# First stage of a two-layer trunk: the modulation of the first layer loaded into the region of v, part of it multiplied on ScalarE and summed in fp32 on TensorE

## The chip, the core and the metric

The kernel runs on one core of one Trainium2 chip. The metric is device time in microseconds (us) of one execution. The kernel before has three runs. The profile shown is of one further execution.

## What is computed

The reference runs two layers, each a token mixer followed by a dense MLP, on x of 1024 tokens by 1024 features in fp32. Ahead of every one of the four sub-layers the input is modulated by a vector c (1024 values) that is the same for all tokens:

```python
def ada_mod(c, w, b):
    m = jax.nn.silu(c) @ w + b                    # w: 1024 x 3072
    shift, scale, gate = jnp.split(m, 3, axis=-1)
    return shift[:, None, :], scale[:, None, :], 1.0 + gate[:, None, :]

h = x * (1.0 + scale) + shift
y = mixer_a(h, ...)        # first layer: uv = gelu(h @ w_in + b_in); u, v = split(uv); ...
x = layer_norm(ALPHA * x + gate * y, ln_g, ln_b)
```

Only the very beginning matters here: `silu(c) @ w` for shift and scale of the first sub-layer, `h`, and the first half of the columns of v = gelu(h @ w_in + b_in).

## The kernel before

**Numbers.** Nearly all matrix products run in the type fp32r. An fp32 operand is split into a high part (a rounded copy) and a low part (the difference), and a product is three matmuls (high times high, high times low, low times high). `split` (L105 to L108) makes the two parts: the copy on ScalarE (A), the difference on VectorE (V).

**The first stage** is the block with `ada0` in `mixer_a` (L495 to L575). It does four things.

1. *The modulation*, `mods(h)` (L502): for each half h of the columns (512 of shift and 512 of scale at once), eight row blocks of 128 rows of `ada_w`, each 512 KB, are loaded into tiles `adaw` with six buffers. VectorE multiplies block k by column k of silu(c) and adds it to the accumulator `adaacc` (L509 for the first block, L511 for the others). The accumulator is then split into `adahi` and `adalo`, and `mod_cols` (L115) sums it over its 128 partitions on TensorE: 16 matmuls against two columns of ones (L119, L120) into a PSUM bank `psa`, once for scale and once for shift. VectorE adds the bias (L124); the result, a few columns, scales and shifts h.
2. *h transposed*, `build_hT` (L221): for a feature block k and up to four row tiles of x, TensorE transposes the tiles into a PSUM bank `pst` (L227), ScalarE applies the modulation (L232) and the result is split into high and low part `hT`.
3. *The weights*, `v_unit` (L466): 512 KB of `a_w_in` are loaded and split into `winv_hi` and `winv_lo`.
4. *The product*, `v_sum(c, i, k)` (L469): three matmuls of 128 x 512 for row tile i and feature block k into the PSUM bank `psv` of that tile. Six banks exist (`mm`); two more (`tr`) serve the transposes and `psa`.

Row tiles are taken in three groups: tiles 0 to 3, tiles 4 and 5, tiles 6 and 7. The feature blocks 0 to 3 need half h=0 of the modulation, the blocks 4 to 7 need half h=1. So the order on TensorE is: group 0-3 with blocks 0 to 3 (48 matmuls), group 4-5 with blocks 0 to 3 (24), then the same two groups with blocks 4 to 7 (48 and 24), then group 6-7 with all eight blocks (48). Each of these sums ends in `v_end` (L478): bias on VectorE, gelu on ScalarE, statistics on VectorE, written into `vz`, the region that holds v for all eight row tiles (8 x 1024 fp32 values per partition).

TensorE has nothing to multiply until the first modulation is there. A burst of 26 matmuls without use (`warm`, L513 to L516) runs from the arrival of block 4 of the first half.

**What sets the order.** A scheduler orders the instructions of each engine ahead of the run: program order is their priority, and an instruction that is marked with `keep_in_program_order` isn't moved against it. In the first stage before, the burst and the transpose of `rows` (L548) are marked; the transposes of x, the low parts and the accumulation on VectorE are not. All loads of the stage are issued by SyncE (SP). A buffer of a pool (or of a tag in it) is taken again when its last reader is done: `adaacc_0`, `adaacc_1` and the x tile 7 share one buffer (tag `gate`).

The rows of ln_g, ln_b, the biases (`rows`, L541 to L544) are loaded between the first x tiles and the second half's blocks, and transposed once (`row_cols`, L546). The bias of the modulation, `ada_b`, is loaded at the start beside c (L74), and both are transposed together (L79).

## Time and profile before

| | us |
|---|---|
| runs | 2681.38, 2685.55, 2686.34 (median 2685.55) |
| the profiled execution | 2684.56 |
| its span in the trace | 2682.9 |

The span runs from the first to the last instruction that the profile shows; 1.66 us of the profiled execution lie outside it. Its mean granted TensorE clock is 0.997 of full speed.

In the answers of the trace, PE is the matmul part of TensorE and PEld its weight loads, which overlap; DVE is VectorE, ACT is ScalarE, SPq the queue of SyncE. A row of the timeline has the start, the duration of the merged run of instructions, engine, line, operation, output <- input, count, and in brackets the idle time before it with what ended that. A row of the windows has the stretch, its length, the busy time of each engine with its count of instructions, the granted clock of TensorE, the share of the DMA engines that was busy, and GB/s.

### The profile page before, as it was taken

To read this page: it belongs to the slowest core of one execution; us is meant where nothing else is said; L and a number is where in the kernel's file an instruction comes from. 1 tells how busy PE (TensorE), PEld (TensorE's weight loads), DVE (VectorE), ACT (ScalarE), POOL (GpSimd) and SP (SyncE) were. 2 spreads that over 40 slices of the span, in tenths; PEclk is the share of its full clock that TensorE was granted. 3 is DMA by queue.
4 is the path that set the end of the run, shared out by engine and by line. 5 is a ranking of instruction groups with operands and counts; after the bars stand their busy time and mean duration, and the time that the engine had idled before them with its cause. 6 is when DMAs were issued, how large, how long until landed. Compare 5 with 4: busy or idle time off the path is not lost.

```text
span 2682.9 us, 36963 instructions
## 1 busy us (share of the span) xinstructions
PE 2646.9 (99%) x13204; PEld 2188.1 (82%) x13204; DVE 1981.9 (74%) x3582; ACT 1382.0 (52%) x2626; POOL 104.4 (4%) x189
## 2 busy tenths in 40 slices
PE   7999999999999999999999999999999999999998
PEld 6888878878888888888888888888877788888887
DVE  5896798787888888555557777776658966677877
ACT  3364475555444564433436666666656655553432
POOL 0000000000000001111110000000010000000000
PEclk9999999999999999999999999999999999999999
DMA  7643347677967645655565554555783654485562
GB/s 276 187 144 102 118 151 242 212 231 263 352 208 257 214 162 196 212 195 179 183 207 157 157 135 131 136 145 140 237 213 113 204 199 157 145 316 190 181 207 83
DMA packets 335069, 505.29 MB, mean 188 GB/s; under 512 B 51692, under 2 KB 168852, under 8 KB 334884
## 3 DMA queue, kind: packets, MB, share of 16 engines
q1 hardware_dynamic: 318500, 444.20, 52.0%
q0 software_dynamic: 16384, 58.73, 6.1%
q8 instruction: 103, 1.69, 0.3%
q14 instruction: 82, 0.67, 0.1%
HBM read 365.92 MB, written 136.92 MB: 187 GB/s over the span
## 4 chain that ended last, share of the span: by engine, by line
PE 69%; issue 17%; DVE 6%; DMA 4%; ACT 2%; POOL 2%; SPq 0%; POOLq 0%; DVEq 0%; ACTq 0%
PE psd L1015 19%; PE psua L853 9%; PE psk L1445 7%; PE psq L1445 6%; PE psuc L853 4%; PE psd_wout L391 3%; PE pv L1614 3%; PE psu L640 3%; PE sc L1534 3%; PE psv L475 3%; DMA adaw<-in_ada_w_dram 3%; PE psub L853 2%; PE pT L1587 1%; POOL v L1321 1%; PE psoa L1818 1%
## 5 line engine op out<-in xcount | busy, mean ns | idle before, releaser
L853 PE MATMUL psua<-right,left 128*128 128x512 f32 x1536 | 365.1, 391 | 1.6 <-ACT part L858 1.2
L1015 PE MATMUL psd<-rhi,lhi 128*128 128x512 f32 x896 | 349.7, 390 | 0.0
L1015 PE MATMUL psd<-rlo,lhi 128*128 128x512 f32 x896 | 348.8, 389 | 0.0
L1015 PE MATMUL psd<-rhi,llo 128*128 128x512 f32 x896 | 348.6, 389 | 0.0
L853 PEld LDWEIGHTS psua<-right,left 128*128 128x128 f32 x1536 | 286.3, 188 | 65.6 <-ACT part L858 3.6
L1556 ACT ACTIVATE p<-p,stat 128x128 f32<-128x128 f32 (+1 forms) x384 | 168.7, 441 | 97.1 <-DVE stat L1554 97.1
L1015 PEld LDWEIGHTS psd<-rhi,lhi 128*128 128x128 f32 x896 | 168.2, 188 | 35.8 <-ACT part L884 0.9
L1015 PEld LDWEIGHTS psd<-rhi,llo 128*128 128x128 f32 x896 | 168.2, 188 | 35.0
L1015 PEld LDWEIGHTS psd<-rlo,lhi 128*128 128x128 f32 x896 | 168.2, 188 | 34.6
L853 PE MATMUL psuc<-right,left 128*128 128x512 f32 x768 | 188.7, 392 | 1.1 <-ACT part L858 1.1
L853 PEld LDWEIGHTS psuc<-right,left 128*128 128x128 f32 x768 | 142.9, 188 | 33.4 <-ACT part L858 2.6
L108 DVE TENSOR_TENSOR pTlo<-pT,pThi 128x512 fp32r<-128x512 f32 (+1 forms) x160 | 99.2, 620 | 76.0 <-ACT pThi L107 75.0
L107 ACT CAST left<-ws 128x512 fp32r<-128x512 f32 x128 | 79.3, 621 | 143.4 <-DVE ws L777 104.6
L108 DVE TENSOR_TENSOR llo<-lraw,lhi 128x1024 fp32r<-128x1024 f32 x112 | 136.1, 1217 | 2.3 <-ACT lhi L107 2.3
L108 DVE TENSOR_TENSOR left<-ws,left 128x512 fp32r<-128x512 f32 x128 | 87.9, 688 | 66.1 <-ACT left L107 63.8
L144 DVE SCALAR_TENSOR_TENSOR adaacc<-adaw,silu_c,adaacc 128x512 f32<-128x512 f32 x140 | 104.4, 746 | 39.4 <-DMA adaw<-in_ada_w_dram 38.7
L1445 PE MATMUL psk<-form_L,wqk_hi 128*128 128x512 f32 x384 | 127.1, 412 | 0.5 <-DVE qlo L108 0.5
L1445 PE MATMUL psq<-form_L,wqk_hi 128*128 128x512 f32 x384 | 126.4, 410 | 0.0
L107 ACT CAST lhi<-lraw 128x1024 fp32r<-128x1024 f32 x112 | 117.1, 1047 | 7.1 <-PE psd L1015 3.3
L1344 PE MATMUL psv<-vrhi,form_S 128*128 128x512 f32 x384 | 119.9, 390 | 0.8 <-ACT vrhi L107 0.5
L1554 DVE CUSTOM_DVE_ANT_0 p<-sc,bias 128x128 f32<-128x128 f32 (+1 forms) x384 | 113.5, 345 | 6.6 <-PE sc L1534 6.2
L107 ACT CAST pThi<-pT 128x512 fp32r<-128x512 f32 (+1 forms) x160 | 84.7, 530 | 61.5 <-PE pT L1587 44.5
(333 smaller groups left out, 6072.6 us busy)
## 6 DMA issues: line engine op xcount, KB each, us to landing
lraw<-forms SPq DMA_DIRECT2D x112, 512.0 KB
adaw<-in_ada_w_dram SPq DMA_DIRECT2D x160, 256.0 KB
up<-in_mlp_w_up_dram SPq DMA_DIRECT2D x64, 512.0 KB
forms<-s SPq DMA_DIRECT2D x128, 256.0 KB
rraw<-in_mlp_w_down_dram SPq DMA_DIRECT2D x64, 512.0 KB
forms<-part SPq DMA_DIRECT2D x96, 256.0 KB
v<-vs POOLq DMA_DIRECT2D x48, 512.0 KB, 3.6
vraw<-in_b_w_qkv_dram SPq DMA_DIRECT2D x42, 512.0 KB
```

The costliest lines, as they stand in the source:

```text
L107: first = A.copy(hi, src) if hi_engine is A else hi_engine.tensor_copy(hi, src)
L108: return first, lo_engine.tensor_tensor(lo, src, hi, op=ALU.subtract)
L144: ins = V.scalar_tensor_tensor(acc[:], raw[:], silu_c[:, k : k + 1], acc[:], ALU.mult, ALU.add)
L391: T.matmul(p[:], stat[a][:, k, o : o + P], u[b][:, w], start=n == 0, stop=n == count - 1)
L475: T.matmul(sums[i][:], hT[half][a_][:, k, o : o + P], units[c, k // 2][b_][:, n : n + HALF], start=k + a_ + b_ == 0, stop=k == KD - 1 and ...
L640: T.matmul(p[:], wu[a_][:, k * P : (k + 1) * P], hT[half][b_][:, k, :], start=k + a_ + b_ == 0, stop=k == KD - 1 and a_ == 1)
L853: T.matmul(acc, w[:, a, k, :], right[p][:, b, k, :], start=p in (1, 2, 5) and k + a + b == 0, stop=k == 3 and a == 1, skip_group_check=True)
L1015: ins = T.matmul(sums[kind, m][:], l[a][:, k, m * P : (m + 1) * P], r[b][:, k, :], start=p in (1, 5, 2, 3) and kp + k + a + b == 0, stop=k ...
L1344: T.matmul(acc, rows[:, m * P : (m + 1) * P], cols_, start=p in (1, 2, 5) and kp + k + a + b == 0, stop=kp == 1 and k == 1 and a == 1, ski ...
L1445: T.matmul(p[:], wu[a][:, k * P : (k + 1) * P], h_op(k, half, b), start=k + c_ == 0, stop=k == KD - 1 and c_ == 2)
L1554: V.tensor_tensor_reduce(out=pr, in0=banks[e][:, sl], in1=st["bias"][:, width - w :], scale=-0.125, scalar=3e38, op0=ALU.add, op1=ALU.min, ...
L1556: A.activation(pr, pr, AF.Exp, bias=nm, scale=-1.0, accum_out=l)
```

## The change

- In the first half, all eight blocks of `ada_w` are loaded into `vz[:, k]`, which is free at that time, so no load waits for a buffer. In the second half the blocks 0 to 5 go to the `adaw` buffers and 6 and 7 to `vz[:, 0]` and `vz[:, 1]`. The weights `winv` 2 and 3 are loaded into `vz[:, 2]` and `vz[:, 3]`.
- In the first half, blocks 6 and 7 are multiplied by their column of silu(c) on ScalarE, in place, and go to TensorE as they are. Blocks 0 to 5 stay on VectorE. The second half stays on VectorE with all eight blocks.
- `total` sums over the partitions in fp32: 8 matmuls of a 128 x 128 block against one column of ones, for each of block 6, block 7 and the accumulator in the first half (24 in all), and for the accumulator in the second half (8). The split of the accumulator (four instructions for each half) and the 16 matmuls of `mod_cols` for each half are gone. `mod_cols` is still used by later stages.
- The burst has 18 matmuls in place of 26 and starts with block 0 in place of block 4.
- `ada_b` is loaded behind the eight blocks and transposed by itself between the sums; the loads of `rows` and their transpose move to the end of the stage.
- The transposes of x, the low parts of h, and VectorE's accumulation of the second half are kept in program order. `in_turn` puts the transposes of a feature block two steps ahead of its matmuls, and the groups 0-3 and 4-5 follow each other in one sequence. The second half's loads of x tiles 0 to 3 come ahead of `winv` 2 and 3.

```diff
-    cols_c = cst.tile([P, KD + 64], F32, name="cols_c")
-    cols_b = cols_c[:, KD : KD + 64]
+    cols_c = cst.tile([P, KD], F32, name="cols_c")
+    cols_b = cst.tile([P, 64], F32, name="cols_b")
+    one = cst.tile([P, 1], F32, name="one")
...
-        nc.sync.dma_start(rows_c[KD : KD + 64, :], ada_b.rearrange("i s (q p) -> (i s) q p", p=P)[:, 0 : 2 * KD, :])
...
-            split(hi, lo, h[:], hi_engine=hi_engines[k % 2])
+            ins = split(hi, lo, h[:], hi_engine=hi_engines[k % 2])
+            if pin_lo:
+                tc.keep_in_program_order(ins[1])
...
+            def in_turn(*runs):
+                todo = [(i0, n, k) for i0, n, ks in runs for k in ks]
+                gens = {(i0, n): rows_of(i0, n)(ks) for i0, n, ks in runs}
+                def rows(m):
+                    if m < len(todo):
+                        next(gens[todo[m][:2]])
+                rows(0)
+                rows(1)
+                yield
+                for m, (i0, n, k) in enumerate(todo):
+                    for i in range(i0, i0 + n):
+                        v_sum(0, i, k)
+                    yield
+                    rows(m + 2)
...
                 def mods(h, between=()):
+                    p = bank("tr", f"psa_{h}")
+                    def total(t, first, last):
+                        for part in range(2):
+                            for k in range(4):
+                                at = 8 * part + 2 * k
+                                T.matmul(p[:, at : at + 1], t[:, part, k * P : (k + 1) * P], one[:],
+                                         start=first and part + k == 0, stop=last and part + k == 4, skip_group_check=True)
                     for k in range(KD):
-                        raw = ada0.tile([P, 2, HALF], F32, name=f"adaw_0_{h}_{k}", tag="adaw", bufs=6)
+                        if h and k < 6:
+                            raw = ada0.tile([P, 2, HALF], F32, name=f"adaw_0_{h}_{k}", tag="adaw", bufs=6)[:]
+                        else:
+                            raw = vz[:, k - 6 * h, :].rearrange("p (t n) -> p t n", t=2)
...
+                        if h == 0 and k > 5:
+                            A.activation(raw, raw, AF.Copy, scale=silu_c[:, k : k + 1])
+                            total(raw, k == 6, False)
...
-                        if h == 0 and k == 4:
-                            A.copy(warm, raw[:, 0, :])
-                            for _ in range(26):
+                        elif k == 0:
+                            tc.keep_in_program_order(A.copy(warm, raw[:, 0, :]))
+                            for _ in range(18):
...
-                    hi, lo = (ada0.tile([P, 2, HALF], F32R, name=f"ada{m}_{h}", tag="adaw", bufs=6) for m in ("hi", "lo"))
+                    if h == 0:
+                        nc.sync.dma_start(rows_b[0:64, :], ada_b.rearrange("i s (q p) -> (i s) q p", p=P)[:, 0 : 2 * KD, :])
+                        pt = bank("tr", "rows_bt")
+                        tc.keep_in_program_order(T.transpose(pt[:, 0:P], rows_b[:], ident[:]))
+                        tc.keep_in_program_order(V.tensor_copy(cols_b[:], pt[:, 0:64]))
+                    total(acc[:], h == 1, True)
...
                 mods(0)
                 x_cols(0, range(4))
+                turns = in_turn((0, 4, first_ks), (4, 2, first_ks))
                 for kp in range(2):
+                    next(turns)
                     v_unit(0, kp)
...
+                then = {n: [lambda: next(turns)] for n in (1, 3, 5, 6, 7)}
                 mods(1, then)
-                x_cols(1, range(6))
+                x_cols(1, range(4))
+                for kp in (2, 3):
+                    v_unit(0, kp, vz[:, kp, :])
+                run(turns)
+                x_cols(1, (4, 5))
                 nc.sync.dma_start(vbias[:], a_b_in[0, D : 2 * D].partition_broadcast(P))
+                row_loads()
+                run(in_turn((0, 4, last_ks), (4, 2, last_ks)))
+                row_cols()
```

More of the change, by code (lines that the diff above doesn't have):

```diff
@@ L219, in in_pair, with build_hT @@
         return lambda k: tuple(t[:, k, :] for t in pair)
-    def build_hT(j, half, tiles, place, ks=range(KD), pinned=False, hi_engines=(A, V), name=None):
+    def build_hT(j, half, tiles, place, ks=range(KD), pinned=False, hi_engines=(A, V), name=None, pin_lo=False):
         name, n_cols = name or f"{j}_{half}", len(tiles) * P
@@ L569, in mixer_a @@
             later(ada_steps(0, GATE, 4) + ada_steps(1, MODS + GATE, 4))
-            gen = rows_of(6, 2)(range(KD))
-            for k in range(KD):
-                advance(gen, k, (6, 7))
-                tick()
+            for n, _ in enumerate(in_turn((6, 2, range(KD)))):
+                if n:
+                    tick()
             for i in (6, 7):
```

63 lines of the change are left out of this document (27 added, 36 removed).

## The prediction

> **What bounds the kernel now.** I read the page first, then the stage by windows, then the three engines' timelines in the first 50 us, then the clock.
>
> ```profile
> span 2682.9 us, 36963 instructions
> ...
> PE 2646.9 (99%) x13204; PEld 2188.1 (82%) x13204; DVE 1981.9 (74%) x3582; ACT 1382.0 (52%) x2626; POOL 104.4 (4%) x189
> ```
>
> TensorE is busy in all but 36 us (2682.9 - 2646.9). A microsecond that the start gives back is kept only if TensorE is packed behind it, so I cut the start into stages:
>
> ```profile
> 8.00:14.00 6.00, 1.14 (x3) 0.95 (x4) 5.51 (x5) 0.62 (x1) 0.00 (x0) 1.00 1.04 380
> 14.00:20.00 6.00, 6.00 (x20) 4.72 (x19) 4.63 (x5) 1.15 (x3) 0.00 (x0) 1.00 1.05 406
> 20.00:26.30 6.30, 5.92 (x40) 5.17 (x38) 3.12 (x6) 4.55 (x6) 0.00 (x0) 0.87 0.95 299
> 26.30:45.90 19.60, 19.02 (x82) 14.92 (x81) 15.21 (x18) 8.05 (x16) 0.00 (x0) 0.95 0.90 336
> 45.90:52.60 6.70, 6.15 (x34) 5.18 (x33) 2.07 (x6) 3.06 (x6) 0.00 (x0) 0.70 0.52 168
> 52.60:72.30 19.70, 19.18 (x82) 15.27 (x81) 9.62 (x17) 9.33 (x18) 0.00 (x0) 0.93 0.60 184
> 72.30:74.50 2.20, 1.08 (x7) 0.56 (x5) 1.91 (x4) 1.92 (x5) 0.00 (x0) 1.00 0.00 0
> ...
> 97.20:212.00 114.80, 114.80 (x535) 95.78 (x534) 101.37 (x172) 52.11 (x77) 0.00 (x0) 1.00 0.55 168
> ```
>
> The 115 us behind the stage are full, so what the stage gains or loses should reach the end one for one. The stage itself has a **front** (to 26.3, the first useful matmul), a first block of 72 matmuls (to 45.9), a **gap** of 6.7 us in which TensorE only sums and transposes, a second block of 72 (to 72.3), and a short gap of 2.2. Until 20 us the DMA engines are full (1.04 and 1.05). What ends the front shows on DVE, ACT and PE:
>
> ```profile
> 9.65 5.26 DVE L511 SCALAR_TENSOR_TENSOR adaacc<-adaw,silu_c,adaacc 128x1024 f32<-128x1024 f32 x4 [0.16 <-DMA adaw<-in_ada_w_dram]
> 15.56 2.60 DVE L511 SCALAR_TENSOR_TENSOR adaacc<-adaw,silu_c,adaacc 128x1024 f32<-128x1024 f32 x2 [0.65 <-DMA adaw<-in_ada_w_dram]
> 18.85 1.29 DVE L108 TENSOR_TENSOR adalo<-adaacc,adahi 128x512 fp32r<-128x512 f32 x2 [0.69 <-ACT adahi L107]
> ```
>
> ```profile
> 12.19 0.62 ACT L513 CAST hT<-adaw 128x512 fp32r<-128x512 f32 x1 [5.64 <-DMA adaw<-in_ada_w_dram]
> 18.20 1.14 ACT L107 CAST adahi<-adaacc 128x512 fp32r<-128x512 f32 x2 [5.39 <-DVE adaacc L511]
> 19.99 1.05 ACT L107 CAST winv_hi<-winv_raw 128x1024 fp32r<-128x1024 f32 x1 [0.66 <-DMA winv_raw<-in_a_w_in_dram]
> ```
>
> ```profile
> 12.86 8.57 PE L516 MATMUL warm<-hT,ones_r 128*128 128x512 f32 x26 [6.83 <-ACT hT L513]
> ...
> 22.75 0.25 PE L119 MATMUL psa<-ones_r,adahi 128*128 128x2 f32 x1
> 22.86 0.25 PE L120 MATMUL psa<-ones_r,adalo 128*128 128x2 f32 x1
> 22.97 0.66 PE L227 MATMUL pst<-ident,x 128*128 128x128 f32 x4
> 23.80 0.66 PE L227 MATMUL pst<-ident,x 128*128 128x128 f32 x4 [0.17 <-DVE ada L124]
> 24.67 1.97 PE L227 MATMUL pst<-ident,x 128*128 128x128 f32 x8 [0.22 <-ACT h L232]
> 26.29 0.78 PE L475 MATMUL psv<-winv_hi,hT 128*128 128x512 f32 x1
> ```
>
> The chain: the last modulation block (its DVE step starts at 15.56 + 1.30 = 16.86, so it has landed by then), the split on ACT and DVE (to 20.1), the sums `psa`, held back by the burst, which ends at 21.4, and 3.2 us from the end of `psa` (22.86 + 0.25 = 23.1) to the first `psv` at 26.29.
>
> **The change, part by part.**
>
> *Loads at once.* Sizes:
>
> ```profile
> adaw<-in_ada_w_dram SPq DMA_DIRECT2D x16, 512.0 KB
> x<-in_x_dram SPq DMA_DIRECT2D x16, 256.0 KB
> ```
>
> The DMA engines are full already, so loading at once moves no more bytes per microsecond; it takes one x load of 256 KB from ahead of blocks 6 and 7. At 0.38 to 0.41 MB per us that is 0.67 us: block 6 lands at 14.9, block 7 at 16.2. `winv` comes at 20.0 as before, having the same bytes ahead of it. `ada_b`, now behind the eight blocks, should land with block 7, ahead of its use.
>
> *Two blocks on ScalarE.* ACT needs about 1.05 for 128x1024 (the `winv_hi` row): block 6 done at 15.95, block 7 at 17.25. DVE, at 1.30 a block, would have ended block 7 at 17.5, so this alone gives some 0.2. It adds 16 matmuls.
>
> *The sum in fp32.* No row shows an fp32 matmul that isn't a transpose. The nearest rows are `psa`: 22.75 to 22.86, 0.11 us from one to the next at full clock. Below, I bound an fp32 one by the same 0.11; above, by the four products of two two-part operands, 0.44, and by twice that at half clock, 0.88. I take **0.18**, under the 0.22 of two loads, near the low row since only one column is streamed.
>
> [...]
>
> *The burst.* 18 matmuls from block 0, which lands four blocks of some 1.35 ahead of block 4 (12.19, the ACT row): near 7. The 26 took 8.57, so 18 take 6 to 7 and end near 14. The sums no longer wait for it, but TensorE then idles. The granted clock:
>
> ```profile
> 21.00:24.60 3.60, 3.29 (x26) 2.72 (x25) 2.23 (x4) 1.85 (x4) 0.00 (x0) 1.00 0.97 297
> 24.60:28.00 3.40, 3.33 (x12) 3.04 (x13) 2.23 (x4) 3.10 (x7) 0.00 (x0) 0.51 0.88 275
> ...
> 45.00:48.50 3.50, 3.02 (x20) 2.40 (x18) 2.09 (x5) 1.14 (x2) 0.00 (x0) 1.00 0.00 1
> 48.50:52.00 3.50, 3.44 (x17) 2.88 (x17) 0.16 (x1) 1.75 (x3) 0.00 (x0) 0.51 0.81 255
> 52.00:55.30 3.30, 3.30 (x11) 2.76 (x11) 1.48 (x3) 3.00 (x6) 0.00 (x0) 0.50 0.98 347
> ```
>
> It halves at 24.6, 3.2 us after the burst's end, and again at 48.5, 2.6 us after the last `psv`; small sums and transposes between don't hold it. At half clock `psa` goes from 0.11 to 0.21:
>
> ```profile
> 48.53 0.35 PE L119 MATMUL psa<-ones_r,adahi 128*128 128x2 f32 x1
> 48.74 0.35 PE L120 MATMUL psa<-ones_r,adalo 128*128 128x2 f32 x1
> ```
>
> [...]
>
> By the two drops, 2.6 and 3.2 us after the last dense matmul, the clock would halve near 17 after a burst that ends at 14; as I can't tell the phase in another run, I allow for 17 to 20.5, in the middle of the sums, and take 18.7.
>
> *Front summed.* 24 fp32 matmuls from 15.95: 15 at 0.18 to 18.7, 9 at 0.36 to 21.9 (at full clock throughout 20.3, halved from 17 on 23.5). With 0.15 for the bias transpose and the 3.2 of before to the first `psv` that is 25.3 against 26.3, **gain 1.0**.
>
> *First block.* Matmuls are 0.23 apart:
>
> ```profile
> 45.00 0.62 PE L475 MATMUL psv<-winv_hi,hT 128*128 128x512 f32 x2
> 45.46 0.39 PE L475 MATMUL psv<-winv_lo,hT 128*128 128x512 f32 x1
> ```
>
> 72 are 16.4 of the 19.6. After: 16.4, plus 16 transposes now between them (two steps of four, four of two; before, the 16 of tiles 0 to 3 lay in the front) at about 0.12 (four in 0.66, overlapped), 1.9, plus the 8 fp32 matmuls of the second half, 1.4, plus 1.7 for a start at half clock (an estimate: 3.4 us at half speed, as 52.0 to 55.3 shows). 21.4 in all: **loss 1.8**.
>
> *The gap.* Split, 16 small matmuls and the transposes behind them go from between the blocks: the sum of the second half lies inside the first block. What stays is one transpose, modulation and split, as in the gap of 2.2 before tiles 6 and 7. I take 2.5 for 6.7: **gain 4.2**. Its cover is that the second half's loads are there: DMA at 0.9 of full in the first block can bring blocks 0 to 7 (4.2 MB) by about 34, and the sum is due near 41.
>
> *Second block.* 16.4 + 1.9 = 18.3 for 19.7, since TensorE comes into it at full clock: **gain 1.4**.
>
> *Orders kept, waits added.* The low parts of h on DVE now stand behind the accumulation steps and, later, behind the two `winv_lo`:
>
> ```profile
> 33.65 1.22 DVE L108 TENSOR_TENSOR winv_lo<-winv_raw,winv_hi 128x1024 fp32r<-128x1024 f32 x1
> ```
>
> A step of DVE is two accumulations and a low part, 2 x 1.30 + 0.65 = 3.25; one of TensorE is 12 x 0.23 + 4 x 0.12 = 3.2. They are even, so DVE can just hold TensorE: **loss 0.5**, kept between 0 and the 3 of a rival. The first accumulation of the second half must also wait for the fp32 sum to leave the shared buffer (21.9), with all later low parts queued behind it on DVE; the first of these is due after 30, so it costs nothing. On SP the four row loads and `ada_b` move back past other issues; nobody waits for the rows until the end of the stage. x tile 7 needs the buffer of the second sum, some 42, which is early enough for its use after 70.
>
> Sum: 1.0 - 1.8 + 4.2 + 1.4 - 0.5 = **4.3 gained**. From the profiled execution (2684.56) that gives 2680.3; its time is 1.0 under the median of the three runs, 2685.55, from which it would be 2681.3. I write 2681.
>
> **The rivals.**
>
> *Dear fp32* (slower). At 0.44, 24 matmuls take 10.6 at full clock (to 26.5) and, with all behind 19 at half clock, to 33.4; the first `psv` comes at 29.9 to 36.8, a loss of 3.6 to 10.5, and the 8 of the second half cost 2.1 more. With -3.9 for the first block and +5.1 for the rest, it is 2.4 to 9.3 lost: 2687 to 2694, middle 2691. It decides from the price at which 32 matmuls eat the 4.3: 0.18 + 4.3/32 = 0.31 each. For it speaks that no `psa` here is fp32; against it that each streams one column.
>
> *Cheap fp32.* At 0.11 and full clock the sums end at 17.25 + 16 x 0.11 = 19.0. Then the weights bind: `winv` lands at 20.0, 1.05 on ACT, 1.22 on DVE: first `psv` at 22.4, gain 3.9; first block loses 1.3. With 4.2 + 1.4 - 0.5 it is 7.7: 2677. It needs the clock to hold until 19.
>
> *DVE takes over.* The kept low parts wait for both `winv_lo` (2.45) and for blocks that land late, so the steps run at DVE's pace; 3.5 lost in place of 0.5, so 1.3 is gained: 2683. For it: DVE is busy 15.2 of 19.6 us in the first block already.
>
> *Not what it says:* loading at once frees nothing, as the DMA engines are full. That removes the 0.67 alone and lies inside these cases.
>
> **How the numbers follow.** Chances: forecast 0.38 (own range 2678 to 2684), dear fp32 0.22, cheap fp32 0.24, DVE 0.16. 0.2% is 5.4 us, about what a measurement of this kernel can tell from no change, so faster means below 2680.2. The forecast has 0.17 of its 0.38 there, cheap fp32 all: 0.41. Slower than 2690.9: 0.16 of dear fp32, and 0.06 for forecast and DVE at worse clocks than taken: 0.22. The rest, 0.37, is within. The range takes in cheap fp32 at its best (2674.5) and most of dear fp32: 2674.5 to 2692.5.
>
> **What would show it.** Right: the first `psv` at 24 to 27; `psa` rows of 128x1 in fp32 some 0.18 apart; the gap between the blocks under 3 us; granted clock near 1.0 through the second block; loads of the first half issued without waits. Wrong: `psa` over 0.31 apart or at half clock; a first `psv` later than 28; `psv` waiting for DVE `hT` inside the first block; or a stage that ends earlier while the end of the span doesn't move.

## The result and the profile after

| | us |
|---|---|
| runs of the changed kernel | 2692.60, 2695.22, 2697.91, 2698.81, 2702.00 (median 2697.91) |
| runs of the kernel before beside them | 2681.38, 2685.15, 2685.55, 2686.24, 2686.34 (median 2685.55) |
| ratio | 1.0051, 95% interval 1.004 to 1.0063 |
| the profiled execution | 2698.81, span 2697.1, mean granted clock 0.993 |

The change makes the kernel slower, by 12.4 us in the medians and 14.2 in the profiled executions. The predicted 2681 and the range to 2692.5 both lie under it.

The page of the changed kernel, in the same two lines as before:

```profile
span 2697.1 us, 37004 instructions
...
PE 2657.6 (99%) x13229; PEld 2197.1 (81%) x13229; DVE 1978.4 (73%) x3579; ACT 1384.7 (51%) x2624; POOL 104.8 (4%) x189
```

TensorE is busy 10.7 us more (2657.6 - 2646.9) and idle 3.5 more. The page has 25 more matmul records (13229 for 13204): an fp32 sum shows as two, so 32 of them are 64 records where the two-part sums were 32, one transpose is new, and the burst has 8 fewer. At the 0.11 of a sum record at full clock 25 records would be some 3 us, so many of the matmuls must also take longer, which points at the clock. The windows of the changed kernel, cut where its stages and its granted clock change (the column behind POOL is the clock):

```profile
6.10:13.25 7.15, 7.10 (x18) 5.27 (x18) 6.05 (x6) 0.00 (x0) 0.00 (x0) 1.00 1.01 363
13.25:15.38 2.13, 0.00 (x0) 0.00 (x0) 0.85 (x1) 1.15 (x1) 0.00 (x0) 1.00 1.05 353
15.38:22.21 6.83, 6.82 (x32) 6.82 (x33) 0.00 (x0) 1.15 (x1) 0.00 (x0) 0.50 1.05 387
22.21:25.62 3.41, 3.41 (x18) 3.41 (x19) 0.22 (x1) 0.00 (x0) 0.00 (x0) 0.50 1.05 387
25.62:30.54 4.92, 2.08 (x10) 1.68 (x9) 1.54 (x5) 3.58 (x6) 0.00 (x0) 0.50 1.05 387
30.54:35.86 5.32, 5.32 (x13) 4.05 (x14) 4.30 (x4) 0.90 (x1) 0.00 (x0) 0.50 1.06 389
35.86:52.94 17.08, 17.08 (x91) 13.87 (x89) 10.40 (x14) 7.96 (x14) 0.00 (x0) 1.00 0.44 159
52.94:56.34 3.40, 0.93 (x6) 0.79 (x7) 2.42 (x3) 0.63 (x1) 0.00 (x0) 1.00 0.90 285
56.34:58.20 1.86, 1.20 (x7) 0.80 (x5) 0.02 (x1) 1.45 (x3) 0.00 (x0) 0.50 0.95 319
58.20:63.17 4.97, 4.97 (x12) 3.91 (x13) 1.37 (x2) 1.25 (x2) 0.00 (x0) 0.50 0.32 119
63.17:79.50 16.33, 16.29 (x80) 12.90 (x79) 8.46 (x15) 9.84 (x17) 0.00 (x0) 1.00 0.29 92
```

The burst ends at 13.25 and TensorE has nothing for 2.13 us. The clock halves at 15.38, just as the sums begin, and stays halved to 35.86, through all 24 sums of the front and 5.3 us of the first block. It halves again from 56.34 to 63.17. In the stage that is 20.5 + 6.8 = 27.3 us at half clock, where the kernel before shows 10.2: 3.4 from 24.65 and 6.8 from 48.55.

TensorE's timeline of the changed kernel (start, duration, line, output <- input, count, idle time before and its cause):

```profile
6.14 7.10 PE L554 MATMUL warm<-hT,ones_r 128*128 128x512 f32 x18 [1.01 <-ACT hT L551]
15.39 6.99 PE L532 MATMUL psa<-one,vz 128*128 128x1 f32 x32 [2.14 <-ACT vz L542]
22.24 0.45 PE L560 MATMUL rows_bt<-ident,rows_b 128*128 128x128 f32 x1
22.48 3.41 PE L532 MATMUL psa<-one,adaacc 128*128 128x1 f32 x16
25.76 1.95 PE L228 MATMUL pst<-ident,x 128*128 128x128 f32 x8
30.54 0.80 PE L478 MATMUL psv<-winv_hi,hT 128*128 128x512 f32 x1 [2.84 <-ACT winv_hi L108]
...
48.44 1.92 PE L532 MATMUL psa<-one,adaacc 128*128 128x1 f32 x16
...
55.41 0.73 PE L478 MATMUL psv<-winv_hi,hT 128*128 128x512 f32 x2 [2.48 <-DVE hT L109]
55.98 1.55 PE L228 MATMUL pst<-ident,x 128*128 128x128 f32 x8
58.20 0.80 PE L478 MATMUL psv<-winv_hi,hT 128*128 128x512 f32 x1 [0.67 <-ACT hT L108]
```

An fp32 sum appears as two matmul records: x32 are the 16 sums of blocks 6 and 7. At half clock one costs 6.99 / 16 = 0.437; at full clock, at 48.44, 1.92 / 8 = 0.24 (the end of the last one included). The first `psv` comes at 30.54 instead of 26.29, **4.25 later**. ScalarE's timeline shows the two products, and what the first `psv` waits for behind the sums: the weights' high part, which ran at 19.99 in the kernel before, stands behind the two steps of h.

```profile
14.19 1.15 ACT L542 ACTIVATE vz<-vz,silu_c 128x1024 f32<-128x1024 f32 x1 [8.10 <-DVE adaacc L547]
15.68 1.15 ACT L542 ACTIVATE vz<-vz,silu_c 128x1024 f32<-128x1024 f32 x1 [0.34 <-DMA vz<-in_ada_w_dram]
26.89 1.63 ACT L233 ACTIVATE h<-pst,ada,ada 128x512 f32<-128x512 f32 x2 [10.07 <-PE pst L228]
28.42 1.12 ACT L108 CAST hT<-h 128x512 fp32r<-128x512 f32 x2
29.45 1.99 ACT L108 CAST winv_hi<-winv_raw 128x1024 fp32r<-128x1024 f32 x2
```

The second loss is at 52.94. The last two `psv` of the second group wait 2.48 us for a low part on VectorE:

```profile
52.66 2.36 DVE L109 TENSOR_TENSOR winv_lo<-vz,winv_hi 128x1024 fp32r<-128x1024 f32 x2 [2.03 <-ACT winv_hi L108]
54.94 0.42 DVE L109 TENSOR_TENSOR hT<-h,hT 128x256 fp32r<-128x256 f32 x1
```

The kept order puts both `winv_lo` ahead of it, and these wait for ScalarE's `winv_hi`. Tiles 6 and 7 start 7.0 late (81.56 for 74.53); the next stage, `psu`, 8.9 (143.32 for 134.46): the gate's sum at 105.62 now waits 0.5 for its input, and some 1.3 more go in smaller pieces that I have not placed. The remaining 5.4 us come later; behind waits near 1370 (1.9 us, for VectorE's `qlo`) and 1980 us (4.2, for a transfer), which are in the kernel before too (0.5 and 2.2), the clock of the changed kernel falls for 3.4 us each time (at 1377.3 and 1984.9), and that of the kernel before does not.

### The profile page after: what moved, and what is told of

Its sections match the earlier page's. It is cut to its first block, busy times and chain, and to the rows that moved or that the text cites. A ratio compares the mean times of both kernels' runs of the same rounds, so it can differ in the third digit from the quotient of the medians.

```text
span 2697.1 us, 37004 instructions
## 1 busy us (share of the span) xinstructions
PE 2657.6 (99%) x13229; PEld 2197.1 (81%) x13229; DVE 1978.4 (73%) x3579; ACT 1384.7 (51%) x2624; POOL 104.8 (4%) x189
## 4 chain that ended last, share of the span: by engine, by line
PE 65%; issue 17%; DVE 7%; DMA 5%; ACT 3%; POOL 2%; SPq 0%; POOLq 0%; DVEq 0%; ACTq 0%
PE psd L1055 17%; PE psua L893 8%; PE psk L1485 7%; PE psq L1485 6%; PE psuc L893 4%; PE psd_wout L394 3%; PE psv L478 3%; PE pv L1654 3%; PE psu L680 3%; DMA adaw<-in_ada_w_dram 3%; PE sc L1574 3%; PE psub L893 2%; PE pT L1627 1%; POOL v L1361 1%; DVE left L109 1%
```

## The experiments

All times are medians beside runs of the kernel before in the same session, for which "before" is given. A single profile turned out to be one draw of the times at which the clock falls. In the two kernels that were profiled twice the first `psv` repeats to 0.3 and 0.4 us, but `psu` only to 2.3 and 4.1, since a halved stretch of 3.4 us comes or goes between runs of one kernel. Differences in `psu` under some 4 us therefore say little. So the table also has the time at half clock, 2 x (1 - mean granted clock) x span, averaged over all runs of a kernel. The clock is on record to 0.001, which is 5.4 us in one run, so only the averages are of use; 5 to 8 us of it stand at the very end of each profile. For the kernel before it is 12.7 to 14.7 us, for the changed one 36.7 in the first session and 34.5 in the repeat.

| kernel | median / before | ratio, interval | first `psv` | `psu` | half clock |
|---|---|---|---|---|---|
| before | | | 26.29 | 134.5 | 13 to 15 |
| changed | 2697.91 / 2685.55 | 1.0051, 1.004 to 1.0063 | 30.54 | 143.3 | 36.7 |
| changed, repeat | 2694.26 / 2682.16 | 1.0047, 1.0034 to 1.0059 | 30.82 | 141.0 | 34.5 |
| 1 burst of 30 | 2693.34 / 2682.32 | 1.0034, 1.0021 to 1.0046 | 28.56 | 140.9 | 28.4 |
| 2 no block on ScalarE | 2686.77 / 2682.32 | 1.0019, 1.0008 to 1.0029 | 24.02 | 136.2 | 27.3 |
| 3 as 2, sums in two parts | 2687.72 / 2682.16 | 1.0017, 1.0008 to 1.0026 | 25.61 | 138.5 | 27.8 |
| 4 weight units later | 2688.87 / 2682.32 | 1.0021, 1.0013 to 1.003 | 31.14 | 139.3 | 26.0 |
| 5 edits 1, 2 and 4 | 2682.50 / 2682.16 | 0.9999, 0.999 to 1.0008 | 23.27 | 130.9 | 14.6 |
| 6 as 5, with filling | 2683.07 / 2682.16 | 1.0005, 0.9996 to 1.0014 | 26.66 | 132.6 | 13.7 |
| 7 loads alone | 2681.10 / 2682.32 | 0.9995, 0.9986 to 1.0003 | 26.08 | 134.1 | 12.1 |
| 8 loads, bias rows | 2682.27 / 2681.74 | 1.0, 0.9991 to 1.0008 | 26.08 | 131.2 | 13.4 |
| 9 loads, kept orders | 2685.64 / 2681.74 | 1.0012, 1.0004 to 1.0021 | 24.99 | 132.3 | 16.1 |
| 9 again | 2685.74 / 2683.15 | 1.0007, 0.9998 to 1.0016 | 25.37 | 136.4 | 16.6 |
| 10 as 9, units later | 2687.23 / 2681.74 | 1.0012, 1.0002 to 1.0022 | 25.79 | 137.0 | 16.6 |
| 11 as 8, burst of 36 early | 2679.24 / 2682.12 | 0.9989, 0.998 to 0.9998 | 24.82 | 131.5 | 18.0 |
| 12 as 11, burst of 18 | 2683.70 / 2683.15 | 0.9998, 0.999 to 1.0007 | 25.74 | 131.2 | 21.9 |
| 13 as 12, the fp32 sums | 2692.16 / 2683.15 | 1.0037, 1.0022 to 1.0053 | 29.90 | 142.6 | 35.3 |
| 14 as 13, burst of 36 | 2682.78 / 2683.15 | 1.0003, 0.9994 to 1.0012 | 26.64 | 134.9 | 18.3 |

**Theory:** the sums are dear because the shortened burst lets the clock fall ahead of them, and one-column sums do not hold it. **Rivals:** an fp32 sum costs 0.4 at any clock; the loads into the region of v cost something; the kept orders are the loss.

### 1. A longer burst

```diff
-                            for _ in range(18):
+                            for _ in range(30):
```

> The changed kernel with a burst of 30 matmuls in place of 18; nothing else differs. Theory (the burst ends at 13.24, TensorE idles 2.1 us, its clock is halved at 15.38 just as the fp32 sums begin, so the sums cost 0.437 each and the first block begins at half clock): the burst now ends at about 16.3, the 24 fp32 sums run at 0.24 each (the price of the second half's eight, 1.92), the first sum of v starts at 26.5 to 27.5 instead of 30.54, the first block gets shorter by 2 to 2.5 (20 instead of 22.4), and the time falls by 5 to 6.5 against the changed kernel. Rival (an fp32 sum of this tile costs 0.4 each whatever the clock, because its two weight loads set it): the first sum of v stays at 30 to 31.5 and the time within 2 of the changed kernel's. Rival (the loads into the region of v are what costs): no difference in time, the clock row changes alone.

TensorE's timeline and, behind it, the windows of this kernel:

```profile
6.17 8.63 PE L554 MATMUL warm<-hT,ones_r 128*128 128x512 f32 x30 [1.01 <-ACT hT L551]
16.24 4.15 PE L532 MATMUL psa<-one,vz 128*128 128x1 f32 x32 [1.43 <-ACT vz L542]
```

```profile
15.96:19.37 3.41, 3.13 (x28) 3.13 (x29) 0.00 (x0) 1.37 (x2) 0.00 (x0) 1.00 1.05 387
19.37:23.91 4.54, 4.54 (x24) 4.54 (x24) 0.23 (x1) 0.00 (x0) 0.00 (x0) 0.50 1.05 387
```

At full clock 14 sums (28 records) take 3.13, 0.22 each, and at half clock the eight from 20.50 on take 3.41, 0.43 each. So the first rival falls: the price follows the clock. But the theory was half wrong as well: in 15.96 to 19.37 TensorE was busy 3.13 of 3.41 us with such sums, and the clock halved at the end of it. The gain was 2.0 at the first `psv`, not 3 to 4, and the ratio went from 1.0047 to 1.0034, 3.5 us and not 5 to 6.5, with intervals that overlap. The wait for the low part behind the first block is still there (2.47).

### 2. No block on ScalarE

```diff
-                        if h == 0 and k > 5:
+                        if h == 0 and k > 7:
...
-                    total(acc[:], h == 1, True)
+                    total(acc[:], True, True)
```

> The changed kernel with all eight row blocks of the first half multiplied on VectorE: no ScalarE copies, eight fp32 sums in place of 24 ahead of the first block. Theory (the 16 sums that the two ScalarE blocks bring, 6.99 us at half clock, are the front's loss): VectorE ends at about 17.0, eight sums at half clock take 3.4, the first sum of v starts at 25 to 26 instead of 30.54 (4.5 to 5.5 earlier), the clock comes back to full earlier in the first block by no more than that, and the time falls by 4 to 6 against the changed kernel. Rival (the 16 sums only fill a wait that something else ends, such as the x columns or the weights): the first sum of v stays within 1 us of 30.5 and the time within 1.5.

TensorE's timeline of this kernel:

```profile
17.53 3.31 PE L532 MATMUL psa<-one,adaacc 128*128 128x1 f32 x16 [0.93 <-DVE adaacc L547]
...
24.02 0.80 PE L478 MATMUL psv<-winv_hi,hT 128*128 128x512 f32 x1 [1.38 <-ACT hT L108]
```

Eight sums instead of 24: the first `psv` is 6.5 earlier, at 24.02, and the time falls from 1.0047 to 1.0019, 7.5 us. VectorE ends its eighth block at 17.5, so the two blocks on ScalarE, with done products at 15.34 and 16.83, spared it 0.7 us at most and brought TensorE 7 us of sums. Against experiment 1, which has about the same time at half clock (27.3 and 28.4), it is 4.7 us faster by the means, though the two intervals overlap: that is near 16 sums at 0.24, 3.8, without more time at half clock.

### 3. The sums in two parts again

The same kernel with split and `mod_cols` for both halves, as before, in place of `total`.

> As the kernel with all eight row blocks on VectorE, but both halves' sums are made as the kernel before makes them: the products' sum split into a high and a low part, 16 fp32r matmuls in place of eight fp32. Theory (the eight fp32 sums at 0.41 each were as dear as the split that they replace): split 2.5 us and 16 sums at 0.2 each on a halved clock, first sum of v at 24.5 to 26.5 against 24.02 with fp32 sums; at 134 us within +0.5 to +3 of that kernel, so +2 to +5 against the kernel before. Rival (fp32 sums are the loss, however few): first sum of v at 22.5 to 23.5 and 1 or more faster than with eight fp32 sums.

The first `psv` comes 1.6 later than in 2 and the time is the same within its interval (1.0017 against 1.0019). Eight fp32 sums are no worse than the split and 16 sums that they replace; they are not the loss.

### 4. The weight units behind the second group

```diff
-                for kp in (2, 3):
-                    v_unit(0, kp, vz[:, kp, :])
                 run(turns)
+                for kp in (2, 3):
+                    v_unit(0, kp, vz[:, kp, :])
```

> The changed kernel with the third and fourth weight units of v written after the last turns of the second block, so that VectorE's kept order has the low part of the fourth column block of tiles 4 and 5 ahead of both weight low parts. Theory (that low part, at 54.94, stands behind the low part of the third unit, which waits for ScalarE's high part, and the idle of 2.48 halves the clock at 56.3): the idle before the last two sums of the first block's second part falls from 2.48 to under 0.6, the gap from 5.26 to about 3, the clock stays at full through the second block, which takes about 19.9 instead of 21.2; the time falls by 3 to 4.5 against the changed kernel. Rival (the wait is taken over by the second half's sums, whose h needs the same units): the gap falls by under 0.7 and the time by under 1. The front stays at 30.5.

VectorE's timeline, and the windows of gap and second block:

```profile
52.13 0.43 DVE L109 TENSOR_TENSOR hT<-h,hT 128x256 fp32r<-128x256 f32 x1 [1.08 <-ACT hT L108]
53.09 1.23 DVE L109 TENSOR_TENSOR winv_lo<-vz,winv_hi 128x1024 fp32r<-128x1024 f32 x1 [0.53 <-ACT winv_hi L108]
```

```profile
53.81:56.57 2.76, 0.88 (x10) 0.64 (x7) 1.04 (x2) 2.28 (x4) 0.00 (x0) 1.00 0.93 318
56.57:75.61 19.04, 19.04 (x90) 15.15 (x91) 10.48 (x18) 11.08 (x19) 0.00 (x0) 1.00 0.47 144
```

The low part comes ahead of `winv_lo`, the wait of 2.48 is gone, the gap is 2.76 instead of 5.26, and the second block runs at full clock in 19.04 instead of 21.3. The ratio falls to 1.0021, 7 us under the repeat's 1.0047, where 3 to 4.5 were expected and `psu` is 4.0 earlier than in the changed kernel and 1.7 than in the repeat. So the edit helps, and the wait, with the second halving behind it, is a cause of the loss; its size in the stage is nearer 4, and where the rest of the 7 went is not shown. It is not always worth as much: in experiment 10 the same edit changed nothing.

### 5 and 6. The three edits together, and filling

> Three edits of the changed kernel together: all eight row blocks on VectorE, a burst of 30, and the third and fourth weight units behind the second block's turns. Theory (the runs of the single edits add up): eight sums at full clock from 17.5, first sum of v at 22.4 to 23.2; the clock still halves about 3.1 after the burst's end, at 19.4 to 20.2, since sums of one column and transposes do not hold it (with the burst of 30 alone it halved at 19.37 in the middle of the sums); the gap between the blocks near 2.6 with no second halving; at 134 us 3 to 4 earlier than the kernel before, and the time 1 to 4 under it. Rival (the single edits' gains overlap, because the earlier first block waits for its x columns or its weights, which land at about 20): first sum of v at 23.6 or later, at 134 us within 2 of the kernel before.

The first `psv` at 23.27 and `psu` 3.6 earlier than in the kernel before are about as expected, the time is not: 0.9999. The change's loss is undone, but nothing of the early start shows at the end. The edits' gains overlap: alone they are 3.5, 7.5 and 7.0 us by the ratios, together 12.9. And 3.6 us of `psu` are within its draws: experiment 8, with the time of the kernel before, has it at 131.2. Experiment 6 has a burst of 32 and ten more matmuls that nothing reads, four behind the sums and six behind the first transposes.

> The combination with a burst of 32 and ten more burst matmuls that nothing reads: four behind the eight sums, six behind the first two groups of transposes, where TensorE waits for ScalarE anyway. Theory (the clock halves when matmuls with 512 columns are missing for about 3 us; sums of one column and transposes count as nothing): no halved clock between 6 and 45 us, sums at 0.24, transposes at 0.13, the first sum of v within 0.7 of the combination's, its first block 2 to 2.5 shorter (19.6 to 20.2), at 134 us 1.5 to 3 earlier than the combination. Rival (the clock falls for another reason, such as a total of work in some window): a halved stretch of 3 us or more remains and the first block is no shorter; then the four extra matmuls cost about 1.

This failed. The last block landed later in that run, the sums started at 18.34, 1.9 after the burst, and the clock halved at 18.69. The filling came too late and made the first `psv` 3.4 later; the time did not change.

### 7 and 8. The loads, and the bias rows

```diff
-                        raw = ada0.tile([P, 2, HALF], F32, name=f"adaw_0_{h}_{k}", tag="adaw", bufs=6)
+                        raw = (vz[:, k, :].rearrange("p (t n) -> p t n", t=2) if h == 0 else
+                               ada0.tile([P, 2, HALF], F32, name=f"adaw_0_{h}_{k}", tag="adaw", bufs=6)[:])
```

> The kernel before with one part of the change alone: the eight row blocks of the first half are loaded into the region of v, with no wait for a buffer. All products stay on VectorE, the sums in high and low parts, the burst of 26 behind the fifth block. Theory (the loads themselves are harmless, and the burst, which ends at 21.4, bounds the front): VectorE ends the last block at about 17 instead of 18.2, the first sum of v starts 0 to 0.7 earlier than 26.29, and the time is within 1.5 of the kernel before, without the +3 at about 1370 us and the +2 to 3 at about 1980 us that the changed kernel shows. Rival (the region of v, or the loads issued together, costs later work in the stage or shifts the later transfers): slower than the kernel before by 3 or more, with the loss behind the first block.

> The kernel with the loads alone, plus the bias rows of the modulations loaded by themselves behind the eight blocks and transposed by a transpose of their own. Theory (it is hidden: the transpose and its copy stand beside VectorE's last products, and the first small load is shorter by half): first sum of v and 134 us within 0.7 of the loads alone (25.7 to 26.8; -1 to +0.4 against the kernel before), time within 1.5 of the loads alone. Rival (the table of biases as a tile of its own costs the later part): the early marks are the same and the median is 1.5 to 5 above the loads alone.

The loads alone, and the loads with the bias rows, put into the kernel before, are within its spread (0.9995 and 1.0). The rival of the loads falls.

### 9 and 10. The kept orders

Experiment 9 has loads and orders of the changed kernel, with burst, products, sums and bias rows of the kernel before. Experiment 10 adds the edit of 4.

> The kernel with the loads alone, plus the part of the change that keeps the steps in order (kept transposes and low parts, the weight units of the second half, the late row loads): burst of 26 behind the fifth block, all products on VectorE, sums in high and low parts, bias rows as before. Theory (the orders by themselves are worth little: the gap between the blocks falls from 6.5 to about 5.3, with the wait of 2.5 for the kept low part in it, the clock halves there as before, and the gate's sums come about 1.6 later between 95 and 105 us): first sum of v at 26 to 27, at 134 us 0 to +3 against the kernel before, time +1 to +5. Rival (the orders are a gain that the front ate): at 134 us 1.5 earlier or more, time at or under the kernel before. For the later part, where all kernels with the orders so far lost 1.5 to 5 by the medians and the loads alone lost nothing: if the orders bring it, the median stands 1.5 or more above what 134 us shows; if it is the bias rows' own load or chance, it does not.

> The same with the third and fourth weight units written behind the second block's turns, so that the kept low part does not stand behind theirs. Theory: as in the changed kernel, where the same edit took 2.5 off the gap and the second halving away, 3.5 to 4.5 earlier at 134 us than with the orders alone, -4 to -1 against the kernel before, and the shortest time here so far if the later part costs nothing: 2678 to 2682 where the kernel before takes 2682. Rival (the wait moves on, since the front is shorter and the weights land no earlier): under 1.5 earlier than with the orders alone.

> The kernel with the loads and the kept orders once more (burst of 26, products on VectorE, high and low parts). Theory (the kept orders leave TensorE idle for about 1.8 more inside the two blocks, waiting for ScalarE's high part of h, and bring the gate's sums 1.6 late): time 1.5 to 5 above the kernel before, as in the first runs (ratio 1.0012). Rival (the first runs were chance): within 1 of it.

Windows from the first `psv` on, at full clock in both kernels: first experiment 8, with the old order, as first block, gap, second block;

```profile
26.08:45.16 19.08, 18.50 (x83) 14.42 (x81) 15.40 (x18) 8.43 (x17) 0.00 (x0) 0.99 0.88 328
45.16:50.59 5.43, 4.45 (x35) 3.65 (x33) 1.84 (x6) 2.54 (x6) 0.00 (x0) 1.00 0.44 148
50.59:69.22 18.63, 18.11 (x84) 14.48 (x83) 10.05 (x17) 9.58 (x18) 0.00 (x0) 1.00 0.66 212
```

then experiment 9, with the kept orders:

```profile
24.99:47.00 22.01, 20.92 (x106) 16.90 (x107) 16.52 (x21) 10.19 (x17) 0.00 (x0) 1.00 0.91 336
47.00:49.48 2.48, 0.88 (x9) 0.64 (x6) 0.01 (x1) 2.00 (x4) 0.00 (x0) 1.00 0.96 333
49.48:68.54 19.06, 19.04 (x90) 15.17 (x91) 9.80 (x17) 10.32 (x18) 0.00 (x0) 1.00 0.37 125
```

The gap falls by 2.95 and the first block grows by 2.93: the work in the gap was needed work (TensorE is busy 4.45 of its 5.43), and it moved. With the second block the orders come out 0.4 longer, and from tiles 6 and 7 to `psu` 1.8 more go (71.25 to 131.18 in experiment 8, 70.57 to 132.29 in 9), 0.5 of it in a wait of the gate's sum for its input. The first `psv` (24.99) and `psu` came earlier than expected, the time as expected: by the ratios the orders cost 2 to 3 us (1.0012 and 1.0007); the second interval touches 1. Experiment 10 missed its expectation: no gain on 9, and no shortest time.

### 11 to 14. Burst and sums in the old order

Experiment 11 is 8 with the burst from the first block on, 36 matmuls long; 12 has 18 there; 13 adds the two blocks on ScalarE and the fp32 sums to 12; 14 is 13 with 36.

> The best parts so far together: loads into the region of v and the bias rows by themselves, products on VectorE, sums in high and low parts, the steps of both blocks in the order of the kernel before, and the burst from the first block on, with 36 matmuls so that it ends at about 17 (in the kernel with the bias rows alone it ended at 19.89 and 26 matmuls stood behind the fifth block). Theory (what the front still waits for there is the burst): products end at 16.2, high and low parts at 18, sums at 18.2 to 20.2, first sum of v at 23 to 24.2 against 26.08; the blocks take what they take in that kernel, give or take one stretch of half clock; mean time 0.5 to 3.5 under the kernel before. Rival (the earlier front is paid back in half clock, since the weights, which land at 19.3 and 20.8, hold the first sums of v apart from the burst by more than 5 us): first sum of v as said, but one or two stretches of 3.4 us more at half clock, and a time within 1 of the kernel before.

> The kernel with the early burst of 36 and no other change but 18 matmuls in the burst: sums in high and low parts, products on VectorE, the order of the kernel before. Theory (the burst ends at 12.5, 5.5 us before the sums, so the clock halves at 15 to 18): sums at 0.21 each, first sum of v at 25 to 26, half clock about one stretch of 3.4 us longer at the start of the first block, time 1 to 3.5 above the kernel with 36, so -1.5 to +1.5 against the kernel before. Rival (the burst's length doesn't matter): the same time as with 36.

> One part alone: loads into the region of v, bias rows by themselves, and, new here, two row blocks on ScalarE, all sums in fp32 and the burst of 18 from the first block; the steps of the two blocks stay in the order of the kernel before. Theory (the fp32 sums of the ScalarE blocks, on a clock that halves under them, are the larger part of the loss): sums from about 15.5 to 26, first sum of v at 28 to 30.5 against 26.29, time 4 to 8 above the kernel before. Rival (the loss is in the kept orders; the sums alone are repaid by the split that goes): time within 2 of the kernel before.

> The kernel with the sums alone and a burst of 36 in place of 18, so that the sums begin right behind it. Theory (half of the sums then run at full clock, 0.24, the rest at 0.44, since sums of one column don't hold the clock): sums from 16.4 to 23.5, first sum of v at 26 to 27.2, 2 to 3.5 earlier than with 18, time 2 to 4 less than with 18. Rival (the price is 0.44 at any clock): no earlier first sum of v.

The timelines of 13 and then 14:

```profile
15.28 6.39 PE L512 MATMUL psa<-one,vz 128*128 128x1 f32 x32 [3.32 <-ACT vz L520]
...
21.78 3.41 PE L512 MATMUL psa<-one,adaacc 128*128 128x1 f32 x16
...
53.10 3.18 PE L512 MATMUL psa<-one,adaacc 128*128 128x1 f32 x16 [3.10 <-DVE adaacc L525]
```

```profile
16.47 3.63 PE L512 MATMUL psa<-one,vz 128*128 128x1 f32 x32
...
20.10 3.27 PE L512 MATMUL psa<-one,adaacc 128*128 128x1 f32 x16
```

Eighteen more burst matmuls bring the first sums from 0.40 each to 0.23, the first `psv` from 29.90 to 26.64, and the ratio from 1.0037 to 1.0003, some 9 us where 2 to 4 were expected. Not all of that is the front: 13 also has a late second accumulation (3.10 idle at 53.10) that 14 does not show. In these two profiles the clock is at half for 27.3 us of the stage with 18 and for 10.2 with 36; half of the 17.1 between them is 8.5, near the whole difference. The pair 11 and 14, with the same half clock (18.0 and 18.3), gives the sums' own price again, net of the split that they spare: 0.0014, 3.8 us, from two sessions and with intervals that overlap a little. Experiment 13, without any kept order of the changed kernel, loses 9 to 10 us, more than the 4 to 8 expected, so the orders are not the main loss.

The burst by itself is worth less: 12, with 18 and two-part sums, has its first `psv` 0.9 later than 11 and the time of the kernel before, 0.0009 or 2.4 us over 11. It takes the short burst and the fp32 sums together to lose 9 to 10. Experiment 11 is the best here, 0.9989 of the kernel before, 0.998 to 0.9998: under 1, if by little, and the lowest of the fifteen kernels in this table, so part of it may be luck. Its first `psv` came later than expected (24.82 for 23 to 24.2). Its windows:

```profile
6.11:16.42 10.31, 10.31 (x37) 8.11 (x37) 8.54 (x8) 0.00 (x0) 0.00 (x0) 1.00 1.04 392
16.42:20.06 3.64, 1.91 (x15) 1.70 (x14) 2.48 (x5) 1.56 (x3) 0.00 (x0) 1.00 1.04 401
20.06:24.82 4.76, 4.37 (x21) 3.42 (x20) 2.81 (x4) 4.04 (x6) 0.00 (x0) 0.50 0.84 261
```

The burst covers the products, the 16 sums in two parts begin 1.6 us behind it, and the clock falls only at 20.06, behind most of them.

### The changed kernel again

> The changed kernel once more, for the part of the loss behind the stage of v: in its profile 8.9 of the 14.2 stand at 134 us and 5.3 come later, at waits for transfers near 1370 and 1980 us. Theory (the later part is jitter of transfers, which every kernel here shows at about 214, 560, 1370, 1450, 1970 us, and which costs about 2 more where a wait is long enough to halve the clock): the first 143 us repeat within 0.7 us (first sum of v at 30.5 to 31.2, +8.5 to +9.5 at the end of the stage), the later part comes out different, anywhere from -2 to +6, and the median of its runs is 9 to 13 above the kernel before. Rival (the change costs the later part by itself): again +1.5 or more at each of the two places and +4 to 6 over both.

The first `psv` repeats within 0.3 (30.82); the end of the stage is +6.5 for +8.9, because the second halving lasted 3.4 us instead of 6.8. The later part is +3.1 (span 9.6 over that of before, less 6.5) instead of +5.4. A wait near 1980 is there in every kernel (a row has who waited for what, the us in total, how often, and the longest), in the changed kernel and its repeat:

```profile
PE sc L1574 <- DMA bk<-qk: 4.2, 1, 4.2
```

```profile
PE sc L1574 <- DMA bk<-qk: 5.0, 1, 5.0
```

and of the kernel before and the loads alone:

```profile
PE sc L1534 <- DMA bk<-qk: 2.2, 1, 2.2
```

```profile
PE sc L1535 <- DMA bk<-qk: 1.3, 1, 1.3
```

In eleven others it is 0.9 to 3.1, and in three (experiments 5, 9 and 9 again) TensorE waits 2.0 there for VectorE's `pTlo` instead. Behind the 4.2 of the changed kernel the clock halved (at 1984.9, for 3.4 us), behind the 2.2 of the kernel before it did not. Neither view is refuted: the later part varies from run to run, and it was a loss both times. A late stage alone doesn't bring the long wait: in experiments 1 and 13, with `psu` at 140.9 and 142.6, it is 1.0 and 1.3. On all engines the order of the instructions is the same behind about 143 us in both kernels, so I know of no way in which the change would lengthen that wait; whether it does stays open.

## Why the prediction was wrong

**The failed step is "Front summed".** It took the loads, the burst's end (14, measured 13.25) and the start of the sums (15.95, measured 15.39) nearly right. The price was too low, 0.18 for a measured 0.22 to 0.24 at full clock and 0.36 for 0.43 at half, but that alone would not have cost the gain: 24 sums at 0.24 from 15.39 would end at 21.2, where the prediction had 21.9. What it got wrong above all was "the clock would halve near 17 ... I take 18.7", with 15 sums at full clock. The clock halved at 15.38, none of the 24 ran at full clock, and they ended at 25.89. By an estimate from these rows (14 sums at 0.24 to 18.7, ten at 0.44), the measured price with the predicted clock gives 23.1: 1.2 of the 4.0 is price, 2.8 the clock. No run shows the 18.7: it lay midway between 17 and an upper bound of 20.5, the author's estimate without a row, and two executions of the changed kernel showed 15.38 and 16.74 in its place. How early the clock fell is in part a draw, but the loss is not: in the repeat, with the fall at 16.74 near the prediction's early bound, the sums ended at 26.17, where its bound was 23.5. Then the 3.2 us "of before" to the first `psv` were 4.65, since transposes and sums before it were at half clock too and `winv_hi` stood behind h on ScalarE. The rival *Dear fp32* came nearest, by luck: its first `psv` at 29.9 to 36.8 takes in the 30.54, and its 2694 is 4 short of the time, but 0.44 was its price at full clock, and is what 0.22 to 0.24 become at half clock. (By its own numbers its 33.4 should be 34.0.)

Each fp32 sum shows two records here (32 for 16 sums), and its 0.24 at full clock is about two of the 0.11 of before.

**Term by term**, in the two profiles: the front loses 4.25 where 1.0 was to be gained; the first block loses 2.8 (22.40 for 19.61; 1.8 was predicted); the gap gains 1.4 (5.26 for 6.70; 4.2 predicted); the second block loses 1.6 (21.30 for 19.74; a gain of 1.4, with 0.5 lost to the orders). That is the 7.0 at tiles 6 and 7. The 1.8 from there to `psu` and the 5.4 behind it the prediction put at nothing, since "what the stage gains or loses should reach the end one for one"; why the later part lost as well stays open.

**The gap** was cut, but "gain 4.2" was not one. Experiments 8 and 9 show 2.95 off the gap and 2.93 on the first block. The prediction had charged the first block 1.8 for transposes, sums and clock; at equal clock the orders' sum over both blocks is a loss of 0.4, where the prediction had gap, blocks and orders together at +3.3.

**"TensorE comes into it at full clock"**, the second block's gain of 1.4, failed through the step *Orders kept*, which priced the low parts behind `winv_lo` at 0.5. *DVE takes over* named that queue; it bit once, for 2.48 us, and with the halving behind it the second block took 21.3 us instead of 18.3. Experiment 4 took both away, and the block still took 19.0, so 18.3 was too short as well.

**Right** were the loads ("loading at once moves no more bytes"): block 7 had landed at 15.68 (predicted 16.2), and alone they are worth nothing that can be told from no change. Three of the named signs of being wrong came: `psa` over 0.31 apart and at half clock, a first `psv` later than 28, and `psv` waiting for VectorE's `hT` inside the first block (2.48 us, ahead of its last two matmuls).

In sum, by the runs: the 16 extra sums on TensorE's path cost some 4 to 5 us between kernels with the same time at half clock (experiments 2 against 1, 14 against 11; loose, since each pair's intervals overlap). The clock goes with most of the loss: over the 16 sets of runs that were made beside the kernel before in one session, the mean time rises by about half a us (0.51) for each us more at half clock (correlation 0.88), so the changed kernel's 21.8 us more would be 11 of its 12. That is a correlation, and the repeat of the changed kernel is one of its points; the pair 13 and 14, which changes the burst alone and whose intervals lie apart, bears it out. The two overlap, since sums at half clock are part of that time. The kept orders come to 2 to 3. These parts overlap and are not a sum.

## What to carry to other kernels

A warm-up burst was worth here what stood right behind it: where it ended 2.1 us ahead of the first sums (the changed kernel) or 3.3 (experiment 13), the clock fell on exactly the work that was to be quick, at 15.38 with sums from 15.39 on and at 15.96 with sums from 15.28 on. Before work is moved to TensorE because it "streams only one column", its time should be counted from a measured row of such work (here 0.22 to 0.24 us a sum at full clock, 0.43 to 0.44 at half), and as time in which the clock may fall, as at 19.37 in experiment 1. And a gap in which TensorE is busy is no gap: moving its work into a full block moved its time as well (2.95 off the gap and 2.93 on the block, experiments 8 and 9).

## What the hardware showed

**Narrow work did not hold the clock.** In the changed kernel TensorE is busy without a pause from 15.39 to 25.89 with fp32 sums of one column and one transpose, and the clock stays at half for all of it (0.50 of full); in experiment 1 it falls at 19.37, after a stretch of 3.41 us with 3.13 us of such sums, and in experiment 14 at 20.24, with TensorE busy for all of the 3.61 us before. In the changed kernel it had fallen 2.13 us after the burst's end, and it came back after 5.3 us of mostly 512-column matmuls (30.54 to 35.86). So it was more than a pause that made the clock fall: in experiment 1 the stretch ahead of the fall was filled to 92%. Where the limit lies was not measured.

**One profile is one draw.** The clock fell at 15.38 in one execution of the changed kernel and at 16.74 in another. Inside the span the stretches at half clock last 3.41 and 6.82 us in the profile of the kernel before, and 20.48, 6.83 and twice 3.41 in that of the changed one; one of 3.41 costs some 1.7 us (an estimate: half of it). So the same gap costs more or less by chance: the gap between the blocks in the old order, with two-part sums, has 6.8 us at half clock in the kernel before and in experiment 7, 3.4 in 11, and none in 8 and 12.
